# Two heads' products with k's low part, each in 64 rows of the TensorE array

## The chip, the cores and the metric

The kernel runs on one core of a Trainium2 chip. The metric is the time of one execution in microseconds on that core. Before the change three runs took 1433.84, 1437.84 and 1439.86 us; their median is 1437.84 us.

## The reference, cut to what matters

A two-layer encoder over 512 positions of width 1024, in float32. Each layer has a mixer (two kinds of attention heads side by side), a cross-attention into 256 memory tokens and a gated MLP with a short convolution. Three of the attentions have heads of width 64, and the change is in their scores:

```
gqa      (layer 0, 8 query heads, 2 key heads):  s = q k^T            512 keys
diff     (layer 1, 4 heads, two scores each):    s1 = q1 k1^T + bias, s2 = q2 k2^T + bias,
                                                 p = softmax(s1) - lam * softmax(s2)   512 keys
na       (layer 1, 8 heads, grid neighbourhood): s = q k^T + bias     256 keys of a block of queries
```

The mLSTM heads of layer 0 and the cross-attentions have heads of width 128; their scores are computed in another way and are not touched.

## The kernel before, in words

The whole kernel is first recorded: every operation becomes an entry with the buffers that it reads and writes. `Recorder.schedule` then places the entries on the engines, by a table of costs (`Recorder.cost`), and `Recorder.trace` issues them in the order that came out. A changed cost therefore changes the order on all engines. Almost every instruction has the line of one helper call in `trace` (L391 before, L398 after); the line says nothing on the operation, and the tiles' names and shapes do: `a` are working tiles of 128x512 in SBUF (80 slots), `w` pairs of weight tiles, `st` staged weights as they come from HBM, `p` the eight PSUM banks of 128x512, `c` columns, `ident` the identity of the transposes.

Full float32 precision comes from products of a high and a low part. A tile x is split into hi (x rounded to the matmul's faster type, fp32r) and lo = x - hi, and a product is summed from hi*hi, hi*lo and lo*hi, each one fp32r matmul of up to 512 columns (`mm3`). The P*V products of the attentions run in float32 without a split; where two heads of width 64 go together, `matmul_halves` (L389) puts one head into columns 0 to 63 of the array and the other into columns 64 to 127.

For heads of width 64 two tricks are used. A tile of queries holds two heads, 64 rows each. `q_stack` makes two tiles of it: `qa` has the first head's hi in rows 0 to 63 and its lo in rows 64 to 127, `qb` the second head's lo in rows 0 to 63 and its hi in rows 64 to 127. `k_stack` makes for each head a tile `kh` with the head's hi in both halves, and a tile `kl` with the head's lo in the half where q's hi stands and zeros (written by GpSimd) in the other half. `scores2` then needs two matmuls over all 128 rows for a head and a block of 128 queries: q with kh gives hi*hi + lo*hi, q with kl gives hi*lo.

The callers are three, each for four pairs of heads and four blocks of 128 queries: `gqa.pair.score` and `na.pair.score` call `scores2` once for each half of a pair, `diff.head.score` twice in one go. `scores2` takes one PSUM bank for each call. `attention` works the pairs one after another: the scores of a pair are computed beside the transposes and P*V products of the pair before, and `merge` mixes in the projections that are due next, so that TensorE has them between the attention's matmuls.

The planner's order: an entry's priority is its place in the recording, moved forward by the boost of its kind (`TUNE`), and at each moment a free engine takes the ready entry of highest priority for which slots are free. A float32r matmul of n columns was reckoned at max(n, 64)/2400 + 0.0027 us, `matmul_halves` at n/600 + 0.12 us.

Of the kernel before, what the change touches and what calls it, by code (L numbers as in the profile page):

```python
# [11 lines left out]
F32 = mybir.dt.float32  # L12
F32R = mybir.dt.float32r
# [4 lines left out]
S = 512  # L18
# [9 lines left out]
ROWS = "p (i c) -> p i c"  # L28
COLS = "p (c i) -> p i c"

NA_KEYS = [(i, (i + 1) % 4) for i in range(4)]
# [98 lines left out]
def _free(v):  # L130
    n = 1
    for d in v.shape[1:]:
        n *= d
    return n


class Recorder:
# [29 lines left out]
    def cost(self, eng, name, args, kw):  # L167
        if name == "load_tables":
            return 1.3, 0.0
        n = _free(args[1] if isinstance(args[1], View) and name not in ("matmul",) else args[0])  # L170
        if eng == "tensor":
            if name == "transpose":
                return 0.11, 0.06
            if name == "matmul_halves":
                return _free(args[0]) / 600.0 + 0.12, 0.06
            n = _free(args[0]) * (1 if args[1].dt == F32R else 4)
            return max(n, 64) / 2400.0 + 0.0027, 0.06
        if name == "dma_start":
            return (0.06 if eng == "sync" else 1.0), 0.0
        if eng == "vector":  # L180
            if name == "reciprocal":
                return 0.06 + n * 0.0065, 0.0
            if name in ("tensor_scalar", "tensor_copy") and n > 8 and args[1].buf.cls != "p":
                return 0.07 + n * 0.00065, 0.0
            if name == "memset":
                return 0.07 + n * 0.0005, 0.0
            return 0.07 + n * (0.00115 if name == "scalar_tensor_tensor" else 0.00104), 0.0
        if eng == "scalar":
            ap = sum(isinstance(kw.get(k), View) for k in ("bias", "scale", "accum_out"))
            return 0.09 + n * 0.000835 + 0.09 * min(ap, 1), 0.0  # L190
        return 0.2 + n * 0.002, 0.0

    def add(self, *alts):
        op = Op()
        op.idx, op.pick, op.placed, op.boost = len(self.ops), None, False, self.boost
        op.alts = [alt + self.cost(*alt) for alt in alts]
        writes, reads = [], []
        for eng, name, args, kw in alts:
            if name == "load_tables":
                writes.append(self.tables)  # L200
                continue
            if isinstance(args[0], View):
                writes.append(args[0].buf)
            reads += [v.buf for v in args[1:] if isinstance(v, View)]
            for k, v in kw.items():
                if isinstance(v, View):
                    (writes if k == "accum_out" else reads).append(v.buf)
            if eng == "scalar" and name == "activation" and args[2] in (AF.Exp, AF.Ln, AF.Silu):
                reads.append(self.tables)
        writes, reads = list(dict.fromkeys(writes)), list(dict.fromkeys(reads))  # L210
        op.preds, op.succs, op.bufs, op.allocs = set(), [], set(reads) | set(writes), []
        for b in reads:
            if b.writer is not None:
                op.preds.add(b.writer)
        for b in writes:
            if b.writer is not None:
                op.preds.add(b.writer)
            op.preds.update(b.readers)
        for b in set(reads) - set(writes):
            b.readers.append(op)  # L220
        for b in writes:
            b.writer, b.readers = op, []
            if not b.live:
                b.live = True
                op.allocs.append(b)
        for b in op.bufs:
            b.left += 1
        if self.hold is not None:
            op.preds.add(self.hold)
        op.preds.discard(op)  # L230
        for p in op.preds:
            p.succs.append(op)
        op.need = len(op.preds)
        self.ops.append(op)
        return op
# [138 lines left out]
    def trace(self, order, home):  # L374
        nc = self.nc
        for n, o in enumerate(order):
            for b in o.allocs:
                pool, width = home(b.cls)
                b.ap = pool.tile([128, width], b.dt, name=f"{b.cls}{b.slot}_{n}", tag=f"{b.cls}{b.slot}")
            eng, fn, args, kw = o.pick[:4]  # L380
            if fn == "load_tables":
                nc.scalar.add_instruction(mybir.InstLoadActFuncSet(
                    name=nc.get_next_instruction_name(), act_func_set_id=args[0], ins=[], outs=[],
                    engine=mybir.EngineType.Activation))
                continue
            r = lambda v: v.resolve() if isinstance(v, View) else v
            if fn == "matmul_halves":
                for h in range(2):
                    nc.tensor.matmul(r(args[0][h * 64:h * 64 + 64]), r(args[1 + 2 * h]), r(args[2 + 2 * h]), **kw)  # L389
                continue  # L390
            getattr(getattr(nc, eng), fn)(*[r(v) for v in args], **{k: r(v) for k, v in kw.items()})  # L391
# [299 lines left out]

def k_stack(K, k, gain=None):

    nc = K.nc
    halves = slice(0, 64), slice(64, 128)
    out = []
    for i, src in enumerate(halves):
        kh, kl = K.ar("kh"), K.ar("kl")
        for dst in halves:
            K.scaled_copy(kh[dst], k[src], gain, src)  # L700
        nc.gpsimd.memset(kl[halves[1 - i]].bitcast(F32), 0.0)
        K.rest(kl[src], k[src], kh[src], gain, src)
        out.append((kh, kl))
    return out


def scores2(K, q2, k2, i, keys=None):

    nc = K.nc
    p = K.ps("s")  # L710
    c = slice(i * 128, i * 128 + 128)
    o, ks = p, k2
    if keys is not None:
        p = p[:, :256]
        o = p.grid(ROWS, 2)
        step = keys[1] - keys[0]
        ks = [k.grid(ROWS, 4)[:, keys[0]:keys[1] + step if step > 0 else None:step, :] for k in k2]
    nc.tensor.matmul(o, q2[:, c], ks[0], start=True, stop=False)
    nc.tensor.matmul(o, q2[:, c], ks[1], start=False, stop=True)
    return p  # L720


@with_exitstack
def trunk(ctx, tc, xT, memT, vec, lam_in, rope, ev_w, ev_o, od_w, od_o, ca_q, ca_kv, ca_o, up, down, na_u, t5, outT):
    K = Kern(ctx, tc)
# [18 lines left out]
    nc = K.nc  # L744
# [227 lines left out]
    def normed(sc, n, bias=None):  # L972
        P, r = softmax(K, sc, n, bias)
        nc.scaled(P, P, r)
        return P

    def gqa(st, ys):
        def pair(j):
            def score(i, half):
                return normed(scores2(K, st["q"][j][half], st["k"][half], i), S)  # L980

            return Head(score, v_two(lambda kt: (st["v"], kt * 128)), take_split(ys), parts=2)

        return attention(K, [pair(j) for j in range(4)])
# [158 lines left out]
    def diff(st, ys):  # L1143
# [12 lines left out]
        def head(h):  # L1156
            def score(i, part):
                b = K.a("t5")
                nc.sync.dma_start(b, t5[h, i])
                P1, r1 = softmax(K, scores2(K, st["q"][h][0], st["k"][h][0], i), S, b)  # L1160
                P2, r2 = softmax(K, scores2(K, st["q"][h][1], st["k"][h][1], i), S, b)
                nc.vector.tensor_tensor(r2, r2, nlam, op=OP.mult)
                nc.scaled(P1, P1, r1)
                nc.vector.scalar_tensor_tensor(P1, P2, r2, P1, op0=OP.mult, op1=OP.add)
                return P1

            def take(y):
                t = K.a("yd")
                nc.copy(t, y)
                qk_norm(t, K.ones, gcol("dg", h), d=128)  # L1170
                yh, yl = K.ar("yh"), K.ar("yl")
                K.split(yh, yl, t)
                ys.append((yh, yl))

            return Head(score, v_one(st["v"], h), take)
# [6 lines left out]
    def na(st, ys):  # L1182


        def pair(j):
            def score(i, half):
                b = K.a("u")[:, :256]
                nc.sync.dma_start(b, na_u[2 * j + half, :, i * 256:i * 256 + 256])
                return normed(scores2(K, st["q"][j][half], st["k"][j][half], i, NA_KEYS[i]), 256, b)

            return Head(score, v_two(lambda kt: st["v"].at(kt, 128 * j)), take_split(ys), parts=2,
                        plan=[(0, (0, 3)), (2, (1, 2)), (1, (0, 1)), (3, (2, 3))],
                        col=lambda q, kt: NA_KEYS[q].index(kt) * 128)

        return attention(K, [pair(j) for j in range(4)])
# [280 lines left out]
```

## Time and profile before

| | |
|---|---|
| median of three runs (lowest, highest) | 1437.84 us (1433.84, 1439.86) |
| the profiled execution | 1435.94 us |
| its span in the trace | 1434.2 us |
| TensorE (PE): busy, matmul records | 1416.3 us, 99%, 6463 |
| VectorE (DVE), ScalarE (ACT), GpSimd (POOL): busy | 965.8 us, 761.6 us, 24.1 us |
| DMA | 135.70 MB, mean 95 GB/s |

PE rows are matmuls and PEld rows are loads of the stationary operand. A matmul's record begins when it is let into the array and overlaps with the next one's, so a matmul's cost in a stream is the distance from one start to the next, not its duration: a record of 0.39 us may stand 0.23 us behind another. A start that is not the first of a merged row is found as the row's start plus its length minus the length of the last record. A float32 matmul leaves two records, an fp32r matmul one. Shapes are written rows*columns of the array in use, then the moving operand.

### The profile page before, as it was taken

What the parts mean: (1) busy time and instruction counts of PE and PEld (TensorE: products, weight loads), DVE (VectorE), ACT (ScalarE), POOL (GpSimd) and SP (SyncE); (2) the same over time, 40 slices, a digit from 0 to 9 for tenths busy, and PEclk for the clock granted to TensorE, in tenths of its full rate; (3) what the DMA queues carried; (4) which work ended last, traced back from release to release, by engine and by line L of the source; (5) the groups of instructions that cost most, each with busy time, mean ns of one, the idle gap of its engine ahead of it and who ended that gap; (6) DMA issues with size and microseconds to landing.
All of it is one profiled execution on the core that took longest, in us unless ns stands there. A gap on an engine that the chain in (4) does not pass through costs nothing. (4 is left out here: it accounts for less than half of the span.)

```text
span 1434.2 us, 17456 instructions
## 1 busy us (share of the span) xinstructions
PE 1416.3 (99%) x6463; PEld 1132.6 (79%) x6463; DVE 965.8 (67%) x1744; ACT 761.6 (53%) x1334; POOL 24.1 (2%) x60
## 2 busy tenths in 40 slices
PE   8999999999999999999999999999999999999998
PEld 5787777786888888888888777877778888888887
DVE  6885588676776777733458797866668777776221
ACT  6476698567444444422346776876664444443111
POOL 1000011000000000000000000000000000000000
PEclk9999999999999999999999999999999999999999
DMA  6222121141333333233352312433213323332321
GB/s 231 66 84 64 63 82 52 60 141 35 103 90 102 96 96 103 82 96 98 92 196 73 124 46 85 147 100 100 92 51 97 100 91 103 89 102 66 140 99 48
DMA packets 48181, 135.70 MB, mean 95 GB/s; under 512 B 5472, under 2 KB 12128, under 8 KB 48096
## 3 DMA queue, kind: packets, MB, share of 16 engines
q1 hardware_dynamic: 48096, 134.60, 29.6%
q8 instruction: 50, 0.82, 0.2%
q14 instruction: 35, 0.29, 0.1%
HBM read 132.48 MB, written 2.10 MB: 94 GB/s over the span
## 5 line engine op out<-in xcount | busy, mean ns | idle before, releaser
L391 PE MATMUL p<-a,w 128*128 128x512 f32 (+1 forms) x4560 | 1053.1, 387 | 0.5 <-DVE w L391 0.5
L391 PEld LDWEIGHTS p<-a,w 128*128 128x128 f32 x4560 | 841.1, 188 | 182.7 <-issue 14.6
L391 DVE TENSOR_TENSOR w<-st,w 128x1024 fp32r<-128x1024 f32 (+2 forms) x246 | 279.0, 1135 | 156.6 <-ACT w L391 154.7
L391 ACT CAST w<-st 128x1024 fp32r<-128x1024 f32 (+2 forms) x219 | 213.8, 978 | 235.5 <-PE p L391 211.8
L391 PE MATMUL p<-w,a 128*128 128x512 f32 x768 | 201.3, 401 | 0.9 <-DVE w L391 0.6
L391 DVE SCALAR_TENSOR_TENSOR a<-a,vec,a 128x504 f32<-128x504 f32 (+3 forms) x324 | 183.2, 589 | 11.5 <-ACT a L391 7.5
L391 DVE TENSOR_TENSOR a<-a,a 128x512 fp32r<-128x512 f32 (+5 forms) x215 | 143.3, 669 | 38.0 <-ACT a L391 34.6
L391 PEld LDWEIGHTS p<-w,a 128*128 128x128 f32 x768 | 140.8, 188 | 34.5 <-issue 5.9
L391 DVE TENSOR_TENSOR a<-p,a 128x512 f32<-128x512 f32 (+2 forms) x127 | 85.4, 672 | 103.4 <-PE p L391 76.0
L391 ACT ACTIVATE a<-a 128x512 f32<-128x512 f32 (+2 forms) x170 | 100.7, 600 | 100.1 <-DVE a L391 99.0
L391 PE MATMUL p<-a,a 128*128 128x512 f32 (+1 forms) x424 | 136.5, 437 | 7.0 <-ACT a L391 6.0
L391 ACT CAST a<-a 128x512 fp32r<-128x512 f32 (+2 forms) x92 | 55.8, 607 | 150.4 <-DVE a L391 148.7
L391 ACT ACTIVATE a<-a,vec 128x512 f32<-128x512 f32 (+2 forms) x139 | 105.9, 765 | 42.1 <-DVE a L391 40.3
L391 ACT ACTIVATE a<-a,c 128x256 f32<-128x256 f32 (+3 forms) x172 | 98.4, 597 | 19.4 <-DVE c L391 19.2
L391 PEld LDWEIGHTS p<-a,a 128*128 128x128 f32 x424 | 78.0, 194 | 32.4 <-ACT a L391 10.1
L391 DVE TENSOR_TENSOR a<-a,p 128x512 f32<-128x512 f32 (+1 forms) x65 | 47.6, 733 | 56.6 <-PE p L391 56.6
L391 PEld LDWEIGHTS p<-ident,a 128*128 128x128 f32 (+2 forms) x474 | 55.5, 140 | 26.4 <-DVE a L391 7.4
L391 PE MATMUL p<-ident,a 128*128 128x128 f32 (+2 forms) x474 | 70.0, 273 | 4.2 <-DVE a L391 3.4
L391 ACT COPY a<-p 128x512 f32<-128x512 f32 (+1 forms) x121 | 61.0, 536 | 18.0 <-PE p L391 17.7
L391 ACT ACTIVATE a<-p,c 128x512 f32<-128x512 f32 (+2 forms) x81 | 48.4, 610 | 24.4 <-DVE c L391 16.8
L391 DVE TENSOR_REDUCE c<-p 128x1 f32<-128x512 f32 (+1 forms) x64 | 34.4, 552 | 12.9 <-PE p L391 11.9
L391 ACT ACTIVATE a<-p 128x512 f32<-128x512 f32 (+1 forms) x58 | 30.9, 534 | 19.6 <-PE p L391 19.4
(73 smaller groups left out, 483.1 us busy)
## 6 DMA issues: line engine op xcount, KB each, us to landing
st<-in_up_dram SPq DMA_DIRECT2D x88, 512.0 KB, 3.5
st<-in_down_dram SPq DMA_DIRECT2D x32, 512.0 KB, 3.6
st<-in_od_w_dram SPq DMA_DIRECT2D x24, 512.0 KB, 3.8
st<-in_ev_w_dram SPq DMA_DIRECT2D x22, 512.0 KB, 3.5
st<-in_ca_kv_dram SPq DMA_DIRECT2D x16, 512.0 KB, 4.3
st<-in_down_dram SPq DMA_DIRECT2D x16, 384.0 KB, 3.1
st<-in_ev_o_dram SPq DMA_DIRECT2D x16, 256.0 KB, 2.6
st<-in_ca_q_dram SPq DMA_DIRECT2D x8, 512.0 KB, 4.2
```

What stands on the lines that cost most here:

```text
L391: getattr(getattr(nc, eng), fn)(*[r(v) for v in args], **{k: r(v) for k, v in kw.items()})
```

## The change

`k_stack` makes one `kl` for two heads: the first head's lo in rows 0 to 63, the second's in rows 64 to 127, without zeros. `scores2` now does both heads of a pair in one call, with two PSUM banks: first both products with `kh` over 128 rows as before, then `matmul_rows`, which issues two matmuls of 64 rows each: qa's rows 0 to 63 with kl's rows 0 to 63, and qb's rows 64 to 127 with kl's rows 64 to 127. `gqa` and `na` make the call at the first half and keep the second bank for the second half. The table of costs gets an entry for `matmul_rows` (one stream of n columns plus 0.13 us), and the constant for a plain matmul goes from 0.0027 to 0.0137 us in fp32r and to 0.006 us in float32.

```diff
+            if name == "matmul_rows":
+                return _free(args[0]) / 2400.0 + 0.13, 0.06
...
-            return max(n, 64) / 2400.0 + 0.0027, 0.06
+            return max(n, 64) / 2400.0 + (0.0137 if args[1].dt == F32R else 0.006), 0.06
...
+            if fn == "matmul_rows":
+                kw = dict(kw)
+                for o, q, h in ((args[0], args[1], slice(0, 64)), (kw.pop("out2"), args[3], slice(64, 128))):
+                    nc.tensor.matmul(r(o), r(q[h]), r(args[2][h]), **kw)
+                continue
...
     halves = slice(0, 64), slice(64, 128)
-    for i, src in enumerate(halves):
-        kh, kl = K.ar("kh"), K.ar("kl")
+    kl = K.ar("kl")
+    khs = []
+    for src in halves:
+        kh = K.ar("kh")
         for dst in halves:
             K.scaled_copy(kh[dst], k[src], gain, src)
-        nc.gpsimd.memset(kl[halves[1 - i]].bitcast(F32), 0.0)
         K.rest(kl[src], k[src], kh[src], gain, src)
-        out.append((kh, kl))
-    return out
+        khs.append(kh)
+    return khs, kl
...
-    nc.tensor.matmul(o, q2[:, c], ks[0], start=True, stop=False)
-    nc.tensor.matmul(o, q2[:, c], ks[1], start=False, stop=True)
-    return p
+    ps = [K.ps("s")[:, :n] for _ in range(2)]
+    os = [p.grid(ROWS, 2) if keys is not None else p for p in ps]
+    for o, q, kh in zip(os, q2, khs):
+        nc.tensor.matmul(o, q[:, c], kh, start=True, stop=False)
+    nc.tensor.matmul_rows(os[0], q2[0][:, c], kl, q2[1][:, c], out2=os[1], start=False, stop=True)
+    return ps
...
+                if half == 0:
+                    both[i] = scores2(K, st["q"][j], st["k"], i)
+                return normed(both[i][half], S)
```

What moves on TensorE is shown at three places. In a row the tile before the arrow is the result, then come the moving and the stationary operand; the last two numbers of a name count allocations.

PE in the gqa stage before, the second block of queries of the first pair: `a_239` and `a_240` are the two heads' kh, `a_1` and `a_23` their kl, `w` are weights of a projection.

```order
L391 MATMUL p_563_814<-a_239_416,a_337_536 128x512
L391 MATMUL p_563_814<-a_1_89,a_337_536 128x512
L391 MATMUL p_343_544<-w_470_698,a_60_190 128x512
L391 MATMUL p_343_544<-w_470_698,a_63_194 128x512
L391 MATMUL p_343_544<-w_470_698,a_60_190 128x512
L391 MATMUL p_570_824<-a_240_418,a_340_540 128x512
L391 MATMUL p_570_824<-a_23_131,a_340_540 128x512
```

The same place now: `a_235` and `a_236` are the kh, `a_246` is the shared kl, L392 are the two matmuls of 64 rows.

```order
L398 MATMUL p_561_813<-a_235_411,a_349_549 128x512
L398 MATMUL p_564_817<-a_236_413,a_352_553 128x512
L392 MATMUL p_561_813<-a_246_424,a_349_549 128x512
L392 MATMUL p_564_817<-a_246_424,a_352_553 128x512
L398 MATMUL p_341_540<-w_468_696,a_59_188 128x512
L398 MATMUL p_341_540<-w_468_696,a_62_192 128x512
```

The two heads' scores stood apart, each complete after two matmuls; now they stand together, the 64-row matmuls behind the two full ones, with full 128-row matmuls ahead of them and behind.

PE in the na stage before, the first block of the first pair, with 256 columns: `a_5978` and `a_5979` are kh, `a_4658` and `a_4673` are kl.

```order
L391 MATMUL p_6098_7832<-a_5978_7682,a_5642_7229 128x256
L391 MATMUL p_6098_7832<-a_4658_5953,a_5642_7229 128x256
L391 MATMUL p_6100_7835<-a_4664_5962,w_6070_7798 128x256 x3
L391 MATMUL p_6100_7835<-a_4672_5973,w_6070_7798 128x256 x3
L391 MATMUL p_6108_7846<-a_5979_7684,a_5648_7237 128x256
L391 MATMUL p_6108_7846<-a_4673_5975,a_5648_7237 128x256
```

The same place now, the shared kl being `a_5949`:

```order
L398 MATMUL p_6052_7813<-a_5925_7652,a_5606_7217 128x256
L398 MATMUL p_6053_7815<-a_5926_7654,a_5612_7226 128x256
L392 MATMUL p_6052_7813<-a_5949_7685,a_5606_7217 128x256
L392 MATMUL p_6053_7815<-a_5949_7685,a_5612_7226 128x256
L398 MATMUL p_6057_7821<-a_4648_5960,w_6022_7777 128x256 x3
```

In the program as it now stands there are 48 such pairs of L392 rows (32 with 512 columns, 16 with 256), and between each pair and the next pair of L392 or of L396 (`matmul_halves`, L389 before) stand at least two full matmuls.

A place that the planner's costs alone move is PE ahead of the first attention, where the gates of the mLSTM are transposed (`ident`, with 36 rows of the array). Here before; `w_353` is a weight tile that VectorE splits just ahead, `a_375` the low part of a square that VectorE makes too:

```order
L391 MATMUL p_300_492<-w_353_556,a_45_169 128x512
L391 MATMUL p_300_492<-w_353_556,a_48_173 128x512
L391 MATMUL p_369_576<-a_375_583,ones_64 128x512
L391 MATMUL p_369_576<-a_162_320,identr 128x512
L391 MATMUL p_300_492<-w_353_556,a_45_169 128x512
L391 MATMUL p_310_506<-w_353_556,a_42_164 128x512
L391 MATMUL p_310_506<-w_353_556,a_44_167 128x512
L391 MATMUL p_310_506<-w_353_556,a_42_164 128x512
L391 MATMUL p_357_561<-a_48_173,w_291_481 128x512
L391 MATMUL p_357_561<-a_45_169,w_291_481 128x512
L391 MATMUL p_393_604<-ident,a_29_143 128x36
```

The same place now:

```order
L398 MATMUL p_365_572<-a_358_562,ones_64 128x512
L398 MATMUL p_355_558<-a_33_150,w_290_478 128x512
L398 MATMUL p_355_558<-a_41_162,w_290_478 128x512
L398 MATMUL p_355_558<-a_43_165,w_290_478 128x512
L398 MATMUL p_355_558<-a_41_162,w_290_478 128x512
L398 MATMUL p_355_558<-a_44_167,w_290_478 128x512
L398 MATMUL p_355_558<-a_47_171,w_290_478 128x512
L398 MATMUL p_355_558<-a_44_167,w_290_478 128x512
L398 MATMUL p_355_558<-a_49_174,w_290_478 128x512
L398 MATMUL p_380_590<-ident,a_25_135 128x36
```

From the first matmul of the next projection (`p_357`, now `p_355`) to the transposes stood 24 matmuls, now 14. The ten that moved behind the transposes are those of `w_353` and of the low part's sum.

VectorE (DVE) at the same place before: the rows of 4x512 and 36x512 are the gates' chain that ends ahead of the transposes.

```order
L391 SCALAR_TENSOR_TENSOR a_29_143<-a_35_153 4x512
L391 TENSOR_TENSOR w_353_556<-st_256_438,w_353_556 128x1024
L391 SCALAR_TENSOR_TENSOR a_29_143<-a_35_153 4x512
L391 TENSOR_TENSOR a_375_583<-a_360_565,a_365_571 128x512
L391 TENSOR_TENSOR a_26_137<-a_26_137,a_29_143 36x512
L391 SCALAR_TENSOR_TENSOR a_35_153<-a_164_323,a_35_153 36x512
L391 TENSOR_SCALAR a_29_143<-a_29_143 36x512
```

And now:

```order
L398 SCALAR_TENSOR_TENSOR a_25_135<-a_27_139 4x512
L398 CAST a_352_553<-a_318_514 64x512
L398 TENSOR_TENSOR a_349_549<-a_318_514,a_349_549 64x512
L398 TENSOR_TENSOR a_352_553<-a_318_514,a_352_553 64x512
L398 TENSOR_TENSOR a_23_131<-a_23_131,a_25_135 36x512
L398 SCALAR_TENSOR_TENSOR a_27_139<-a_163_321,a_27_139 36x512
L398 TENSOR_SCALAR a_25_135<-a_25_135 36x512
L398 TENSOR_TENSOR a_379_588<-a_353_555,a_358_562 128x512
L398 TENSOR_TENSOR a_384_595<-a_27_139,a_376_584 128x512
L398 TENSOR_TENSOR w_363_569<-st_255_437,w_363_569 128x1024
```

The split of the weight tile and the square's low part stood inside the gates' chain and now stand behind it; a cast of 64x512 has come ahead of its end.

## Rows read from the trace of the kernel before

**Rows 1.** The page: busy engines; granted clock over 40 slices.

```profile
PE 1416.3 (99%) x6463; PEld 1132.6 (79%) x6463; DVE 965.8 (67%) x1744; ACT 761.6 (53%) x1334; POOL 24.1 (2%) x60
...
PEclk9999999999999999999999999999999999999999
```

**Rows 2.** Waits of PE: total us, times, longest.

```profile
PE p L391 <- ACT a L391: 6.7, 5, 5.5
PE p L391 <- DVE a L391: 5.7, 9, 1.0
PE p L391 <- DVE w L391: 1.1, 2, 0.6
PE p L391 <- DVE c L391: 0.2, 1, 0.2
```

**Rows 3.** Stretches: length, PE, PEld, DVE, ACT, POOL busy, clock, DMA.

```profile
100.00:200.00 100.00, 100.00 (x509) 72.71 (x508) 65.27 (x131) 71.73 (x151) 5.60 (x14) 1.00 0.22 70
...
800.00:1000.00 200.00, 197.25 (x998) 150.82 (x997) 153.45 (x395) 148.12 (x344) 0.52 (x1) 1.00 0.31 100
```

**Rows 4.** Timeline of PE, full matmuls of 512 and 256 columns: start, us.

```profile
399.67 4.70 PE L391 MATMUL p<-a,w 128*128 128x512 f32 x20
...
922.09 1.96 PE L391 MATMUL p<-a,w 128*128 128x256 f32 x15
```

**Rows 5.** Groups of PE by shape: busy us, mean ns.

```profile
L391 PE MATMUL p<-a,w 128*128 128x512 f32 x4368 | 1025.5, 391 | 0.5 <-DVE w L391 0.5
...
L391 PE MATMUL p<-a,w 128*128 128x256 f32 x192 | 27.6, 284 | 0.0
L389 PE MATMUL p<-a,a 128*64 128x512 f32 x64 | 16.6, 613 | 0.0
```

**Rows 6.** Timeline of PE around one run of 36-row transposes.

```profile
65.80 0.61 PE L391 MATMUL p<-a,w 128*128 128x512 f32 x2
66.34 0.93 PE L391 MATMUL p<-ident,a 36*128 36x36 f32 x12
67.21 0.73 PE L391 MATMUL p<-w,a 128*128 128x512 f32 x2
```

**Rows 7.** The same view around one run of 32-row transposes.

```profile
732.73 0.84 PE L391 MATMUL p<-w,a 128*128 128x512 f32 x3
733.50 0.43 PE L391 MATMUL p<-ident,a 32*128 32x32 f32 x4
733.86 0.73 PE L391 MATMUL p<-w,a 128*128 128x512 f32 x2
```

**Rows 8.** Timeline of PE around one matmul_halves (L389), gqa stage.

```profile
110.31 0.61 PE L391 MATMUL p<-a,w 128*128 128x512 f32 x2
110.86 0.65 PE L389 MATMUL p<-a,a 128*64 128x512 f32 x2
...
110.86 1.08 PE L389 MATMUL p<-a,a 128*64 128x512 f32 x4
111.86 0.73 PE L391 MATMUL p<-a,w 128*128 128x512 f32 x2
```

**Rows 9.** Timeline of PEld there, the loads behind it.

```profile
111.86 0.30 PEld L391 LDWEIGHTS p<-a,w 128*128 128x128 f32 x2 [0.81 <-issue]
112.20 0.19 PEld L391 LDWEIGHTS p<-a,w 128*128 128x128 f32 x1
```

**Rows 10.** Timeline of all engines ahead of the gates' transposes.

```profile
61.12 1.19 DVE L391 TENSOR_TENSOR w<-st,w 128x1024 fp32r<-128x1024 f32 x1
...
62.37 0.96 PE L391 MATMUL p<-w,a 128*128 128x512 f32 x3 [0.60 <-DVE w L391]
63.59 1.29 DVE L391 TENSOR_TENSOR a<-a,a 128x512 fp32r<-128x512 f32 x2
...
64.33 0.49 PE L391 MATMUL p<-a,ones 128*128 128x512 f32 x1 [1.00 <-DVE a L391]
...
71.88 0.42 DVE L391 CAST a<-a 64x512 fp32r<-64x512 f32 x1
```

More of the change, by code (lines that the diff above doesn't have):

```diff
@@ L206, in add @@
                 if isinstance(v, View):
-                    (writes if k == "accum_out" else reads).append(v.buf)
+                    (writes if k in ("accum_out", "out2") else reads).append(v.buf)
             if eng == "scalar" and name == "activation" and args[2] in (AF.Exp, AF.Ln, AF.Silu):
@@ L692, in k_stack @@
 def k_stack(K, k, gain=None):
-    nc = K.nc
     halves = slice(0, 64), slice(64, 128)
-    out = []
-    for i, src in enumerate(halves):
-        kh, kl = K.ar("kh"), K.ar("kl")
+    kl = K.ar("kl")
+    khs = []
+    for src in halves:
+        kh = K.ar("kh")
         for dst in halves:
             K.scaled_copy(kh[dst], k[src], gain, src)
-        nc.gpsimd.memset(kl[halves[1 - i]].bitcast(F32), 0.0)
         K.rest(kl[src], k[src], kh[src], gain, src)
-        out.append((kh, kl))
-    return out
+        khs.append(kh)
+    return khs, kl
 def scores2(K, q2, k2, i, keys=None):
     nc = K.nc
-    p = K.ps("s")
+    khs, kl = k2
     c = slice(i * 128, i * 128 + 128)
-    o, ks = p, k2
+    n = S
     if keys is not None:
-        p = p[:, :256]
-        o = p.grid(ROWS, 2)
+        n = 256
         step = keys[1] - keys[0]
-        ks = [k.grid(ROWS, 4)[:, keys[0]:keys[1] + step if step > 0 else None:step, :] for k in k2]
-    nc.tensor.matmul(o, q2[:, c], ks[0], start=True, stop=False)
-    nc.tensor.matmul(o, q2[:, c], ks[1], start=False, stop=True)
-    return p
+        khs, kl = ([k.grid(ROWS, 4)[:, keys[0]:keys[1] + step if step > 0 else None:step, :] for k in ks]
+                   for ks in (khs, [kl]))
+        kl = kl[0]
+    ps = [K.ps("s")[:, :n] for _ in range(2)]
[4 more added lines that the diff above has]
+    return ps
 @with_exitstack
@@ L978, in pair @@
         def pair(j):
+            both = {}
             def score(i, half):
-                return normed(scores2(K, st["q"][j][half], st["k"][half], i), S)
+                if half == 0:
+                    both[i] = scores2(K, st["q"][j], st["k"], i)
+                return normed(both[i][half], S)
             return Head(score, v_two(lambda kt: (st["v"], kt * 128)), take_split(ys), parts=2)
@@ L1159, in score @@
                 nc.sync.dma_start(b, t5[h, i])
-                P1, r1 = softmax(K, scores2(K, st["q"][h][0], st["k"][h][0], i), S, b)
-                P2, r2 = softmax(K, scores2(K, st["q"][h][1], st["k"][h][1], i), S, b)
+                s1, s2 = scores2(K, st["q"][h], st["k"][h], i)
+                P1, r1 = softmax(K, s1, S, b)
+                P2, r2 = softmax(K, s2, S, b)
                 nc.vector.tensor_tensor(r2, r2, nlam, op=OP.mult)
@@ L1185, in pair @@
         def pair(j):
+            both = {}
             def score(i, half):
@@ L1188, in score @@
                 nc.sync.dma_start(b, na_u[2 * j + half, :, i * 256:i * 256 + 256])
-                return normed(scores2(K, st["q"][j][half], st["k"][j][half], i, NA_KEYS[i]), 256, b)
+                if half == 0:
+                    both[i] = scores2(K, st["q"][j], st["k"][j], i, NA_KEYS[i])
+                return normed(both[i][half], 256, b)
             return Head(score, v_two(lambda kt: st["v"].at(kt, 128 * j)), take_split(ys), parts=2,
```

## The prediction

> **What bounds the kernel now.** I read the page first, then the waits of PE, then stretches of the timeline. The page has PE busy for 1416.3 of 1434.2 us and the granted clock at its upper level, 2.4 GHz, in every slice [rows 1]; DVE and ACT are busy for two thirds and a half. PE's waits come to 6.7 + 5.7 + 1.1 + 0.2 = 13.7 us [rows 2], so 1% of the span is all that better order could ever give. The stretch of the gqa attention (100 to 200 us) has no idle PE at all, the one with diff and na (800 to 1000) 200.00 - 197.25 = 2.75 us [rows 3]. So what a matmul takes in PE's stream goes into the time nearly one to one, and the question is what the new form of the product takes there. The projections run at a steady pace: 20 matmuls of 512 columns fill 4.70 us, the last record lasts 0.39, so (4.70 - 0.39) / 19 = 0.227 us each; with 256 columns (1.96 - 0.28) / 14 = 0.120 us [rows 4, 5].
>
> **What is removed.** For a pair of heads and a block of queries two full matmuls with kl go. There are 4 pairs by 4 blocks in each of the three attentions: 16 in gqa and 16 in diff with 512 columns, 16 in na with 256. Removed are 2 x 0.227 = 0.454 us in 32 places and 2 x 0.120 = 0.240 us in 16 places, 14.5 + 3.8 = 18.4 us.
>
> **What is added.** In each of those 48 places stand two matmuls that use 64 rows of the array, between full ones; no two of these places touch. The trace has no such pair, but it has what stands nearest: the transposes of the gates, 36 rows high, and those of the norms, 32 rows high, both between full matmuls. I take the price of going into a smaller tiling and back from them.
> - Going in. The last full matmul begins at 65.80 + 0.61 - 0.39 = 66.02, the first 36-row transpose at 66.34 [rows 6], 0.32 us later and not 0.227: 0.09 more.
> - Coming out. From the first transpose to the next full matmul it is 67.21 - 66.34 = 0.87 us for twelve [rows 6] and 733.86 - 733.50 = 0.36 us for four [rows 7]. Eight transposes are thus 0.51, 0.064 each, and 0.36 - 4 x 0.064 = 0.10 us is not transposing.
> - The weights. The second full matmul after the run begins at 67.21 + 0.73 - 0.39 = 67.55, 0.34 after the first: 0.11 more than the steady pace. The loads show why: behind the change the next load begins 0.30 - 0.19 = 0.11 us after the first one [rows 9], so the load of 128 columns, elsewhere beside the stream of the matmul before, stands alone.
>
> There and back is 0.09 + 0.10 + 0.11 = 0.30 us. One `matmul_halves` (tiling by columns) checks it: from the last full matmul before, 110.31 + 0.61 - 0.39 = 110.53, to the second behind, 111.86 + 0.73 - 0.39 = 112.20, it is 1.67 us [rows 8], less two full ones 1.21 us. Its float32 product is 512 / 600 = 0.85 us by the planner's rate, 0.36 is left: 0.30 and some 0.06 for loading its own 64 columns of weights with the array empty. It also shows that two tiles of the array do run side by side: four records take 1.08 us, two 0.65 [rows 8].
>
> A 64-row pair loads 128 columns of fp32r weights for each matmul, 0.11 us in the open if both go together, then streams 512 columns at 2.4 GHz, 0.21 us, the second matmul 0.01 behind the first. That makes 0.09 + 0.11 + 0.21 + 0.01 + 0.10 + 0.11 = 0.63 us against 0.454, 0.176 more; with 256 columns the stream is 0.11, the pair 0.52 against 0.240, 0.28 more. The sum is 32 x 0.176 + 16 x 0.28 = 5.6 + 4.5 = 10.1 us more.
>
> Both ends of it. From below, the pair's own weights come in for nothing: 0.52 and 0.41 us, 32 x 0.066 + 16 x 0.17 = 4.8 us more. From above, the two loads go one after the other, 0.11 more for each of the 48: 15.4 us more. I take the middle, since the load of rows 9 is of the same type and width. (The table of costs has 0.13 us beside the stream; it is a reckoning, and the same table's 0.12 for `matmul_halves` stands against the 0.36 just found.)
>
> The Trainium skill, TensorEngine Tiling (Array Packing), Tiling Modes, says that a change of tiling mode drains the engine and a change of tile alone does not, and gives no figure. The drains in rows 6 to 8 agree, but the rows have more than the rule: the open loads on both sides are half of the price. By the drain alone the sum would be -0.4 us, and that is a rival below.
>
> **What lies beside it.** Where PE waits anyway a longer matmul costs nothing: of the 2.75 us idle in the stretch of diff and na I let a third go, -0.9 us; in gqa there is no cover. The 18 half-tile memsets on POOL are gone; POOL is busy for 24.1 us of the span and nothing of this is late, so nothing. A tile less for each pair of key heads (9 of the 80 slots): nothing. The first head's softmax now waits for the second head's product and the pair, 0.2 + 0.6 us later than before; it is DVE's reduction or add that waits, behind it its casts and the low parts of weights for the projections. DVE is busy 65 of 100 us in gqa [rows 3], so I count nothing; without that slack it would be up to 0.8 us for each of the 12 pairs or heads that begin an attention step, 9.6 us at most.
>
> **The new costs.** They move the order everywhere. Where they move most, ahead of the gates' transposes, PE before waited 0.60 us for a weight split of 1.19 us and 1.00 us for a low part [rows 10]. Now the transposes come ten matmuls earlier, 10 x 0.227 = 2.3 us, and the gates' chain loses the split and one low part, 1.19 + 1.29 / 2, but gains a cast of 0.42 [rows 10]: 1.4 us earlier. The two old waits become one that is 2.3 - 1.4 = 0.9 us longer. Between -1.6 (all gone) and +0.9 I take +0.9. Elsewhere I count nothing, between -5 and +5.
>
> **The sum.** 10.1 - 0.9 + 0.9 = +10.1 us. Against the profiled execution (1435.94 us, span 1434.2 and 1.7 around it) that is 1446.0, against the median of the runs, 1.9 above it, 1447.9. I take 1447, 0.6% slower, with 1442 to 1452 as the range of this case by the ends above.
>
> **The rivals.**
> - No price for the change. Loads and drains of the 64-row matmuls go under the neighbours' streams, and a pair takes 0.227 + 0.01 = 0.24 us, or 0.13: gain 32 x 0.217 + 16 x 0.11 = 8.7 us, 1428 us, faster. For it: two tiles do run together in rows 8. Against it: rows 6 to 8, four kinds of places of one price. It decides from 0.45 us for a pair downwards. The Trainium skill, TensorE: Matmul & The Clock Gate, Part 3, has this rule: a pack takes one matmul and about 4 ns for each further tile; its figures are for packs by themselves, and no run here shows one between full matmuls at that price.
> - The drain alone: 0.09 + 0.21 + 0.01 + 0.10 = 0.41 and 0.30 us, 32 x -0.044 + 16 x 0.06 = -0.4 us, 1436.5. Against it: the 0.11 us of rows 6 and 9 behind each change.
> - Not side by side. If the two 64-row matmuls stream one after the other, as fp32r might ask: 32 x 0.213 + 16 x 0.107 = 8.5 us more, 1455.5 us. The float32 halves of rows 8 speak against it, but they split columns, not rows.
> - The order gains. With matmuls reckoned at 227 ns, as rows 4 have them, the planner's clock fits PE better. Of the 13.7 us of waits one of 5.5 is the kernel's start; if 6 of the other 8.2 go, it is 1441. Against it: what it gained would have to be spread over 16 small waits [rows 2], which the planner already places by its priorities and not by its clock alone.
>
> **How the numbers follow.** The forecast has 0.56, no price 0.09, the drain alone 0.10, one after the other 0.10, the order 0.15. A difference under 0.5%, 7.2 us (1430.6 to 1445.0), is no change that a measurement here can tell. Of the forecast's 0.56 about 0.13 lies under 1445.0. Faster: 0.09. Same: 0.13 + 0.10 + 0.15 = 0.38. Slower: 0.43 + 0.10 = 0.53. The range 1434 to 1456 takes in the drain alone and leaves out the first rival and the upper part of the third, with what the runs' own scatter adds.
>
> **What would show it.** In the profile after: 96 records of 64 rows at L392, two by two some 10 ns apart (right) or 0.2 apart (third rival); the first 0.32 us behind the last full matmul; from it to the next full one 0.42 us with 512 columns and 0.31 with 256; the second full one 0.34 behind the first. PE's busy time up by 9 to 10 us, in the attention stages alone; the MLPs as before. The wait at the gates' transposes one of about 2.4 us. The prediction is wrong if the first full matmul comes 0.23 us behind the pair, or if waits of PE elsewhere change by more than 5 us.

## The result, and the profile after

The changed kernel took 1448.38 us (median of four runs, 1447.88 to 1448.68) beside 1436.69 us for the kernel before: a ratio of 1.0085, 95% interval 1.007 to 1.010. It is slower by 11.7 us; 1447 was predicted, with 1434 to 1456 as the range. The profiled execution took 1447.88 us, its span 1446.2. Busy times and PE's waits, from the page and the view of waits, beside [rows 1, 2]:

```profile
PE 1428.0 (99%) x6463; PEld 1122.1 (78%) x6463; DVE 965.2 (67%) x1743; ACT 767.9 (53%) x1335; POOL 13.6 (1%) x42
```

```profile
PE p L398 <- ACT a L398: 8.1, 5, 5.6
PE p L398 <- DVE a L398: 5.2, 11, 0.9
PE p L398 <- DVE w L398: 0.5, 1, 0.5
```

PE is busy 11.7 us longer, DVE as long as before, and ACT 6.3 us longer, but still for little more than half of the span. PE's waits sum to 13.8 us against 13.7. The time is in PE's own stream. Here is a pair of 512 columns (gqa) and one of 256 (na) on the timeline of PE, then the loads (PEld) around the first:

```profile
114.57 0.62 PE L398 MATMUL p<-a,a 128*128 128x512 f32 x2
115.12 0.50 PE L392 MATMUL p<-a,a 64*128 64x512 f32 x2
115.55 0.73 PE L398 MATMUL p<-a,w 128*128 128x512 f32 x2
...
916.25 0.40 PE L398 MATMUL p<-a,a 128*128 128x256 f32 x2
916.58 0.38 PE L392 MATMUL p<-a,a 64*128 64x256 f32 x2
916.89 0.50 PE L398 MATMUL p<-a,w 128*128 128x256 f32 x2
```

```profile
115.12 0.19 PEld L392 LDWEIGHTS p<-a,a 64*128 64x128 f32 x2 [0.36 <-issue]
115.55 0.30 PEld L398 LDWEIGHTS p<-a,w 128*128 128x128 f32 x2 [0.24 <-issue]
115.89 0.19 PEld L398 LDWEIGHTS p<-a,w 128*128 128x128 f32 x1
```

The starts are found as in [rows 6, 8]. The last full matmul begins at 114.57 + 0.62 - 0.39 = 114.80, the pair at 115.12 (0.32 later), both its matmuls within 0.01 us; the next full one begins at 115.55 (0.43) and the second at 115.55 + 0.73 - 0.39 = 115.89 (0.34). From 114.80 to 115.89 it is 1.09 us; less two full matmuls the pair took 0.63 us where 0.454 was, 0.18 more. With 256 columns the same reckoning gives 0.505 against 0.240, 0.265 more. The other places agree: the next matmul begins 0.42 to 0.44 us behind the pair in all 32 places of 512 columns and 0.31 to 0.32 us behind it in all 16 of 256. The two loads of the pair fill 0.19 us together, so they go side by side, but nothing else streams meanwhile. Over 32 and 16 places that is 5.8 + 4.2 = 10.0 us.

### The profile page after: what moved, and what is told of

It is laid out like the page before. It is cut to its first block, busy times and chain, and to the rows that moved or that the text cites. A ratio compares the mean times of both kernels' runs of the same rounds, so it can differ in the third digit from the quotient of the medians.

```text
span 1446.2 us, 17407 instructions
## 1 busy us (share of the span) xinstructions
PE 1428.0 (99%) x6463; PEld 1122.1 (78%) x6463; DVE 965.2 (67%) x1743; ACT 767.9 (53%) x1335; POOL 13.6 (1%) x42
## 4 chain that ended last, share of the span: by engine, by line
PE 93%; ACT 3%; DVE 2%; issue 1%; DMA 0%; SPq 0%; DVEq 0%
PE p L398 90%; ACT a L398 3%; DVE a L398 2%; PE p L396 2%; PE p L392 1%; ACT w L398 0%; DMA a<-in_xT_dram 0%; DVE c L398 0%; DVE w L398 0%; SPq L398 0%; ACT c L398 0%; DVEq L1491 0%; DVEq L398 0%
## 5 line engine op out<-in xcount | busy, mean ns | idle before, releaser
L398 ACT CAST w<-st 128x1024 fp32r<-128x1024 f32 (+2 forms) x230 | 224.9, 979 | 253.8 <-PE p L398 225.6
L398 DVE SCALAR_TENSOR_TENSOR a<-a,vec,a 128x504 f32<-128x504 f32 (+3 forms) x324 | 183.3, 589 | 14.1 <-ACT a L398 10.1
L398 DVE TENSOR_TENSOR a<-a,a 128x512 fp32r<-128x512 f32 (+4 forms) x215 | 143.1, 669 | 49.2 <-ACT a L398 46.5
L398 PE MATMUL p<-a,a 128*128 128x512 f32 (+1 forms) x328 | 114.9, 457 | 6.3 <-ACT a L398 5.9
L398 PEld LDWEIGHTS p<-a,a 128*128 128x128 f32 x328 | 60.5, 194 | 29.2 <-ACT a L398 9.5
L398 DVE CUSTOM_DVE_ANT_0 a<-p,a 128x512 f32<-128x512 f32 (+1 forms) x64 | 34.2, 552 | 12.1 <-PE p L392 10.9
```

## The experiments

Ratios are to the kernel before, run on the same chip, with 95% intervals. A time in us beside a ratio is the difference of the medians on that chip; two changed kernels, which mostly ran on different chips, are compared by their ratios. A passage means going into the smaller tiling and back. The first four keep the changed kernel's order.

**Full rows.** The products with the shared low tile use all 128 rows.

```diff
-                for o, q, h in ((args[0], args[1], slice(0, 64)), (kw.pop("out2"), args[3], slice(64, 128))):
-                    nc.tensor.matmul(r(o), r(q[h]), r(args[2][h]), **kw)
+                for o, q in ((args[0], args[1]), (kw.pop("out2"), args[3])):
+                    nc.tensor.matmul(r(o), r(q), r(args[2]), **kw)
```

> The kernel after, in the same order to the last instruction, with the shared low tile of k; but each of the two products with it uses all 128 rows of the array. (The rows of the other head add a product of two low parts, which the reference does not have.) Theory, the change of tiling is what costs: each pair of 512 columns goes from 0.634 to 0.454 us, each of 256 from 0.505 to 0.240, 32 x 0.180 + 16 x 0.265 = 10.0 us less than the kernel after, 1438.4 us, and every record behind a product with the low tile 0.23 (0.12) us behind the one before. Rival, the pairing of two heads and the new order cost the time: 1448 us, as after.

Measured 1438.93 us, 1.0027 (1.0016 to 1.0039): 1.0085 - 1.0027 is 8.3 us gone. The same place of gqa on its timeline:

```profile
112.62 0.62 PE L398 MATMUL p<-a,a 128*128 128x512 f32 x2
113.08 0.62 PE L392 MATMUL p<-a,a 128*128 128x512 f32 x2
113.53 1.29 PE L398 MATMUL p<-a,w 128*128 128x512 f32 x5
```

All starts are 0.23 apart again. Since no instruction has moved, the two traces can be set against each other record by record: 3.0 us go in gqa, 2.3 in diff, 3.6 in na, 8.9 in all where 10 was expected. About 0.6 us less than expected went in each of diff and na; 0.3 of it is a new wait in na, the rest is in no wait that the profile names. The change of tiling is shown to be most of the loss. The rest of the way to 1436 is not in it.

**One of two.** The second head's 64-row matmul is left out.

```diff
-                for o, q, h in ((args[0], args[1], slice(0, 64)), (kw.pop("out2"), args[3], slice(64, 128))):
+                for o, q, h in ((args[0], args[1], slice(0, 64)),):
+                    kw.pop("out2")
...
-    for o, q, kh in zip(os, q2, khs):
-        nc.tensor.matmul(o, q[:, c], kh, start=True, stop=False)
+    for o, q, kh, last in zip(os, q2, khs, (False, True)):
+        nc.tensor.matmul(o, q[:, c], kh, start=True, stop=last)
```

> The kernel after in the same order, but the second head's 64-row product with the low tile is left out (that head's scores lack it); the first head's stays. Theory, the two stream side by side and the price is that of going there and back: 48 x 0.003 us less, 1448.3 us, the same as after. Rival, the second product takes time of its own: one stream less for each pair, 32 x 0.213 + 16 x 0.107 = 8.5 us less, 1440 us.

Measured 1447.71 us, 1.0091 (1.0075 to 1.0107). A lone 64-row matmul takes what two take:

```profile
114.22 0.62 PE L399 MATMUL p<-a,a 128*128 128x512 f32 x2
114.77 0.50 PE L393 MATMUL p<-a,a 64*128 64x512 f32 x1
115.20 0.72 PE L399 MATMUL p<-a,w 128*128 128x512 f32 x2
```

It begins 0.32 us behind the last full matmul, and the next full one 0.43 us behind it. So the two do run side by side, and the price is the passage.

**No low product.** Both 64-row matmuls are left out.

```diff
-                for o, q, h in ((args[0], args[1], slice(0, 64)), (kw.pop("out2"), args[3], slice(64, 128))):
-                    nc.tensor.matmul(r(o), r(q[h]), r(args[2][h]), **kw)
+                kw.pop("out2")
...
-        nc.tensor.matmul(o, q[:, c], kh, start=True, stop=False)
+        nc.tensor.matmul(o, q[:, c], kh, start=True, stop=True)
```

> The kernel after in the same order, but both products with the low tile of k are left out in all 48 places. Theory, what a matmul takes in PE's stream goes into the time one to one: 32 x 0.634 + 16 x 0.505 = 28.4 us less than after, 1420 us. Rival, VectorE and ScalarE are close behind and take over: under half of it, 1434 us or more.

Measured 1430.27 us, 0.9969 (0.9959 to 0.9978): 1.0085 - 0.9969 is 17 us less than the kernel after, not 28. Both theories had a number and the truth lies between. Its waits and the stretch of diff and na (columns as in [rows 3]):

```profile
PE p L397 <- ACT a L397: 11.3, 9, 5.6
PE p L397 <- DVE a L397: 7.6, 15, 0.9
PE p L397 <- DVE c L397: 1.3, 3, 0.5
PE p L397 <- DVE w L397: 0.3, 1, 0.3
```

```profile
800.00:1000.00 200.00, 193.82 (x953) 144.47 (x953) 157.53 (x399) 151.05 (x346) 0.00 (x0) 1.00 0.30 93
```

PE waits for 20.5 us in all, in the kernel after for 13.8; in this stretch it is idle for 6.2 us, in the kernel after for 1.6. The named waits are thus 6.7 us of what is missing; 4 us more are missing from PE's busy time, which fell by 24.4 us (1428.0 to 1403.6), and no run says where they went. With this order the time that the tiling adds to PE counts nearly in full (full rows), and the time of the whole product, taken away from PE, does not. The order was not planned anew for the shorter stream.

**Full rows in na alone.**

```diff
+                na = args[0].shape[1] == 2
...
+                    h = slice(0, 128) if na else h
```

> The kernel after in the same order; only in the neighbourhood attention (256 columns, 16 places) the products with the shared low tile use all 128 rows, with the added product of two low parts there. Theory, a change of tiling has one price whatever the columns: 16 x 0.265 = 4.2 us less than after, 1444.2 us. Rival, the price is in the long streams of gqa and diff: 1448 us.

Measured 1445.71 us, 1.0070 (1.0056 to 1.0084). The times alone do not part it from the kernel after, since the intervals overlap; the records do. Record against record 3.5 us go in na. 1.6 us come back behind it, where the granted clock fell in this execution (see the end). The price is in the short streams too.

**Two blocks at a time in na.** A new function `scores2_two` does the four full products of two blocks and then their two pairs, so four 64-row matmuls stand together, in half as many places.

```diff
...
-                if half == 0:
-                    both[i] = scores2(K, st["q"][j], st["k"][j], i, NA_KEYS[i])
+                if half == 0 and i % 2 == 0:
+                    both[i], both[i + 1] = scores2_two(K, st["q"][j], st["k"][j], i, NA_KEYS[i:i + 2])
```

> The kernel after; in the neighbourhood attention the scores of two blocks of queries are done at once, in the two halves of the two banks, so that two 64-row pairs stand together and 8 goings into the smaller tiling go instead of 16. Theory, the price belongs to going there and back: two pairs take 0.505 + 0.12 = 0.63 us in place of 1.01 if the second pair's weights load beside the first pair's stream, 0.72 if in the open: 8 x 0.38 = 3.1 or 8 x 0.30 = 2.4 us less than after, 1445.3 to 1446 us. Rival, each pair has its price wherever it stands: 1448 us.

Measured 1446.54 us, 1.0070 (1.005 to 1.009), about 2 us less than the kernel after, which is too little for the two intervals to tell. The records decide. Two views of one place, up to the first pair and from the second on:

```profile
918.07 0.52 PE L398 MATMUL p<-a,a 128*128 128x256 f32 x3
918.52 0.39 PE L392 MATMUL p<-a,a 64*128 64x256 f32 x2
...
918.74 0.28 PE L392 MATMUL p<-a,a 64*128 64x256 f32 x2
918.95 0.51 PE L398 MATMUL p<-a,w 128*128 128x256 f32 x2
```

The first pair begins 0.21 behind the last full one, the second 0.22 behind the first, the next full one 0.21 behind that, and the second full one at 918.95 + 0.51 - 0.28 = 919.18, 0.23 later. That is 0.87 us; less two full matmuls of 0.120 it is 0.63 us for two pairs, as expected if the second pair's weights load beside the first's stream. The price belongs to the passage, and a second pair on the same passage costs 0.12. The Trainium skill, TensorEngine Tiling (Array Packing), Tiling Modes, has it that a change of the mode drains the engine and a change of the tile does not; the 0.22 us between the pairs agrees. Two full pairs cost 0.48, so even so it does not pay.

**The planner's constants alone, in the kernel before.**

```diff
-            return max(n, 64) / 2400.0 + 0.0027, 0.06
+            return max(n, 64) / 2400.0 + (0.0137 if args[1].dt == F32R else 0.006), 0.06
```

> The kernel before, and of the change only the two constants of the planner (0.0137 and 0.006 us in place of 0.0027); scores and tiles as before. With all 128 rows and the order of the changed kernel the time was still 3.0 us above the kernel before, of which a stretch at a lower clock was 1.6. Theory, the rest is the order that the new constants make: 1437 to 1439 us, with one longer wait ahead of the gates' transposes as in the kernel after. Rival, it comes from doing two heads at once: 1436 us, the same as before. If the constants are of use by themselves: under 1433 us.

Measured 1443.08 us, 1.0043 (1.0028 to 1.0058): 6.8 us slower, outside all three expectations. From its page and its waits:

```profile
PE 1420.8 (99%) x6463; PEld 1131.0 (78%) x6463; DVE 963.2 (67%) x1735; ACT 770.3 (53%) x1343; POOL 22.6 (2%) x60
```

```profile
PE p L391 <- ACT a L391: 7.8, 4, 5.7
PE p L391 <- DVE a L391: 6.9, 13, 1.1
PE p L391 <- DVE c L391: 0.9, 2, 0.8
PE p L391 <- DVE w L391: 0.5, 1, 0.5
```

PE's waits are 16.1 us, only 2.4 more than before. Another 4.5 us are in PE's busy time (1420.8 for 1416.3, with as many records and the clock at 1.00), so another order costs time also where the profile names no wait.

**The old constant in the kernel after.**

```diff
-            return max(n, 64) / 2400.0 + (0.0137 if args[1].dt == F32R else 0.006), 0.06
+            return max(n, 64) / 2400.0 + 0.0027, 0.06
```

> The kernel after with the planner's old constant (0.0027 us) for plain matmuls; the 64-row pairs stay and are planned as in the kernel after. Theory, the tiling is the price and the constants at most 1.5 us: 1446 to 1449 us, pairs of 0.63 and 0.51 us in the records. Rival, the new constants are what costs: 1440 us or less.

Measured 1446.06 us, 1.0065 (1.0049 to 1.0081). The tiling stays most of the loss.

**Neither tiling nor constants.** Full rows, old constants, the product planned as two full matmuls.

```diff
-                return _free(args[0]) / 2400.0 + 0.13, 0.06
+                return 2 * (_free(args[0]) / 2400.0 + 0.0027), 0.06
```

> Two heads at once with the shared low tile, all 128 rows for both products with it (the rows of the other head add a product of two low parts), and the planner's old constants, the product with the low tile planned as two full matmuls. Neither the tiling nor the new constants are in it. If doing two heads at once is free: 1435 to 1438 us. If it costs by itself: 1440 us or more.

Measured 1437.15 us, 1.0009 (0.9999 to 1.0019). Doing two heads at once costs nothing that can be told, at most 2.7 us by the interval.

**The pair's true price in the plan.**

```diff
-                return _free(args[0]) / 2400.0 + 0.13, 0.06
+                return _free(args[0]) / 2400.0 + 0.42, 0.06
-                return _free(args[0]) / 600.0 + 0.12, 0.06
+                return _free(args[0]) / 600.0 + 0.36, 0.06
```

> The kernel after, only the planner is told what the trace shows: 0.42 us beside the stream for a 64-row pair in place of 0.13, 0.36 for a product of two halves in place of 0.12. Theory, the sum is set by PE's stream and the order has little left to give: 1447 to 1449 us. Rival, the planner's too short pairs make the waits: 1445 us or less.

Measured 1454.95 us, 1.0127 (1.0110 to 1.0144): 1.0127 - 1.0085 is 6 us slower than with the wrong price, against both theories. PE's waits are 16.9 us against 13.8.

**Three more constants in the kernel before** (0.0027 for fp32r becomes 0.0047, -0.008 or 0.03).

```diff
-            return max(n, 64) / 2400.0 + 0.0027, 0.06
+            return max(n, 64) / 2400.0 + (-0.008 if args[1].dt == F32R else 0.0027), 0.06
```

> The kernel before; of the planner's table only the constant of an fp32r matmul goes from 0.0027 to 0.0047 us (float32 stays). Theory L, a lottery: the planner's other numbers fit the one order that came out before, and any other order loses some us, so a change by 2 ns costs about as much as the change by 11 did (1443.1 us): 1439 to 1445 us. Theory M, the longer a matmul is reckoned, the later the planner lets the other engines feed it: 2 of 11 parts of 6.8 us, 1437.5 us.

> The kernel before with an fp32r matmul reckoned 10.7 ns shorter instead of longer (constant -0.008 us in place of 0.0027). Theory L: 1439 to 1445 us, as any other order. Theory M: 1430 to 1434 us, faster than both kernels.

> The kernel before with an fp32r matmul reckoned 27 ns longer (constant 0.03 us). Theory L: 1439 to 1446 us. Theory M: 1450 us or more.

Measured 1441.84 us, 1.0032 (1.0020 to 1.0043); 1432.71 us, 0.9967 (0.9956 to 0.9979); 1463.55 us, 1.0182 (1.0168 to 1.0196). Waits of PE, first of the short, then of the long constant:

```profile
PE p L391 <- ACT a L391: 5.8, 1, 5.8
PE p L391 <- DVE a L391: 3.7, 9, 0.9
```

```profile
PE p L391 <- DVE a L391: 13.2, 18, 3.8
PE p L391 <- ACT a L391: 12.4, 15, 5.4
```

Behind the wait at the kernel's start (5.8) PE waits for ACT no more when a matmul is reckoned short; reckoned long, it waits for both. Short, as before, 11 ns longer (there float32 3 ns longer too), 27 ns longer: -3.9, 0, +6.8, +27 us. The lottery falls with the ends, which lie outside its range. The step of 2 ns does not fit the line: +5.2 us, where theory M has about 1 and the lottery 2 to 8. Its profiled execution ran 10 us at the lower clock (6.8 us are shown at the end, 3.4 more stand at 332.7 us), an estimated 5 us lost, and all its six runs have a mean granted clock of only 0.996 to 0.998. Runs of the kernel before on that chip at 0.996 to 0.998 took 1438.1 to 1439.6 us, these 1439.8 to 1442.3. So some 2 to 3 us are left for the order itself. Why the clock is lower in all runs of this order is open. The short constant is faster than both kernels; on the changed kernel it was not tried, only the old one was.

## Why the prediction was right

- **What bounds.** Right upwards: 10 us added to PE came out as 8.3 to 8.9 us (full rows) and PE's waits did not move. Downwards it does not hold (no low product), which the text did not say. That the 13.7 us of waits are all that order could ever give is too narrow: with the same records at full clock PE was busy for 1414.7 us with the short constant and for 1420.8 us with the new constants alone, so order also changes the busy time.
- **The pair.** 0.63 and 0.52 us predicted, 0.63 and 0.505 measured; the parts too: 0.32 going in, 0.43 and 0.31 to the next full matmul, 0.34 behind it. The transposes of [rows 6, 7] and the load of [rows 9] were the right neighbours (rows 6 to 8 hold three kinds of places, not the four that the text counts). The middle between the ends, not the low one, was right because the pair's own weights do load in the open.
- **What lies beside it.** A third of 2.75 us, 0.9, was counted as cover. Idle PE in the stretch of diff and na went from 2.75 to 1.61 us:

```profile
800.00:1000.00 200.00, 198.39 (x973) 142.19 (x973) 146.31 (x386) 145.78 (x339) 0.00 (x0) 1.00 0.26 81
```

- **The gates' transposes.** One wait of 2.4 us was predicted; it became two, 1.86 + 0.69 = 2.55 us. The constants bring them: with the new ones alone the waits there are 1.26 + 1.04 = 2.30 us, with neither tiling nor constants 0.82 + 0.77 = 1.59, as before the change. The sum is right, since the transposes still start when VectorE's chain ends. The first of the two waits, for ScalarE, was not foreseen; as far as the rows tell it only takes part of the time that PE would have stood there:

```profile
61.08 0.50 PE L398 MATMUL p<-a,ones 128*128 128x512 f32 x1 [1.86 <-ACT a L398]
...
64.14 0.91 PE L398 MATMUL p<-ident,a 36*128 36x36 f32 x12 [0.69 <-DVE a L398]
```

- **The new costs elsewhere.** Counted at nothing; this term was too small. Full rows with new and with old constants (the planned price of the pair differs too) are 1.0027 - 1.0009 = 0.0018 apart, 2.6 us, though their intervals overlap a little. Of this 0.9 was counted at the gates; the other 1.7 us are about what the forecast of +10.1 lacked against the +11.7. PE's busy time shows the same: forecast 9 to 10 us more, measured 11.7.
- **The rivals.** No price, the drain alone and one after the other all fall by the records above. The order rival had the wrong sign: reckoning 227 ns, as the trace has it, made the order worse and not better. Why a planner with truer numbers orders worse is not settled. What is shown is that PE then waits more for ACT and DVE, by 2.4 us, and is busy longer, by 4.5 us (the constants alone). That the constants cost 6.8 us alone and 2.6 with two heads at once is also left open.

## What to carry to other kernels

A small tiling of the array between full matmuls is paid by the passage, so count passages before streams: here 0.30 us there and back and 0.11 for the first load, against 0.23 saved. It can pay only where several small products stand together. By the prices found here two pairs of 512 columns on one passage would take 0.63 + 0.22 = 0.85 us (for the second a stream of 0.21 and 0.01 between its matmuls) against 0.91 for four full matmuls, and with 256 columns it would take four pairs, 0.51 + 3 x 0.12 = 0.87 against 0.96. These are estimates; no run has either. A planner's cost for the bounding engine is a knob on the order, not a measurement to be made true; move it both ways on the chip.

## What the hardware showed beside this

The granted clock falls in the middle of some executions. In the kernel with full rows PE had waits of 0.9 and 0.3 us among transposes at the start of the second cross-attention; then ten records of float32 matmuls took 4.64 us, where the kernel after took 3.24 for the same ten:

```profile
1036.27 0.92 PE L398 MATMUL p<-ident,a 128*128 128x128 f32 x4 [0.31 <-DVE a L398]
1036.98 4.64 PE L398 MATMUL p<-a,a 128*128 128x256 f32 x10
```

The stretches of the two kernels, the clock third from the end:

```profile
1036.90:1040.40 3.50, 3.50 (x10) 2.31 (x9) 1.12 (x5) 2.94 (x10) 0.00 (x0) 0.57 0.01 2
```

```profile
1046.50:1050.00 3.50, 3.50 (x15) 2.12 (x14) 2.21 (x10) 3.50 (x13) 0.00 (x0) 1.00 0.01 2
```

A mean of 0.57 is nearly all at 1.2 GHz, and with the transposes just ahead it cost 1.6 us. The kernel after had the same waits there and kept 2.4 GHz in its profiled execution. In the kernel with the constant 0.0047 PE was busy for 0.75 of 3.0 us up to the first of the gates' transposes and then ran 6.8 us at the lower level:

```profile
60.00:63.00 3.00, 0.75 (x6) 0.47 (x6) 2.87 (x6) 2.14 (x4) 0.00 (x0) 1.00 0.00 0
63.00:69.80 6.80, 6.80 (x25) 5.47 (x24) 5.88 (x11) 3.30 (x5) 0.00 (x0) 0.50 0.27 81
69.80:76.00 6.20, 6.20 (x29) 5.10 (x28) 3.02 (x5) 1.40 (x2) 0.00 (x0) 1.00 0.30 85
```

So behind some waits of PE more is lost than their length. That the wait brings the fall is not shown, since the kernel after had the same waits and no fall. The scatter of one kernel comes in good part from this: the kernel before took 1433.3 to 1436.6 us in runs with a mean granted clock of 1.000 and 1439.3 to 1440.1 in those with 0.996. Comparisons of single runs within a few us must allow for it.
